# Token shift of the delta rule: two VectorE passes and an accumulating transfer in place of a copy and three passes

## The chip, the cores and the metric

The kernel runs on one core of a Trainium2 chip. The metric is the time of one launch in microseconds on the device, the median of several runs. TensorE does the matrix products, VectorE, ScalarE and GpSimd the work element by element, and SyncE and the queues of ScalarE and GpSimd issue transfers. Each engine, and each queue, takes its instructions in order; they wait for one another through semaphores.

## What is computed

Two blocks follow one another on 256 tokens of 1024 columns: a first block of attention and a mixture of experts, and a second block of two layers, each with three mixers. One of these is a delta rule (RWKV-7). Its inputs r, k, v and two narrow ones are shifted: each token's row is mixed with the row of the token ahead of it, by a weight mu of its own for each column.

```python
prev = jnp.pad(shift_cols, ((0, 0), (1, 0), (0, 0)))[:, :-1]
shifted = shift_cols + rwkv_mu[l] * (prev - shift_cols)
r, k, v, wl, al = split_cols(shifted, RWKV_SIZES)
```

For the first token prev is zero. r, k and v have 512 columns each, and the two narrow ones 64 each, 128 together.

## The kernel before

The 256 tokens lie on 128 partitions as two tiles (TT = 2): a tensor of 512 columns is 128 x 1024 numbers, token t on partition t modulo 128 in tile t // 128. One token further on is therefore one partition further on, and from partition 127 of the first tile to partition 0 of the second. [...]

The shifts are made in `shift_mix` (L1722). It is called four times in each layer: from `mix_in` for the narrow pair (mx, n = 128), and from `shifted` for k, r and v (n = 512). `shifted` loads the row mu by SyncE (`bc_row`), has `copy_chunk` compute the 512 columns p on TensorE and bring them out of PSUM with ScalarE (L1480), and calls `shift_mix` with the buffer prev. There a GpSimd memset (L1725) clears the first token's row, three transfers from ScalarE's queue (`Q_SHIFT = "scalar"`, L1727 and L1728: 112 partitions, 15 partitions and the one row that changes tile) copy p into prev one token on, and three VectorE passes (L1729 to L1731) form prev − p, times mu, plus p. Then prev and mu are given back to the slots from which they were taken, and others use the space.

Around that, TensorE streams the second block's other weights. Each 512-column weight tile is split in two parts for TensorE: wh on ScalarE (L460) and wl on VectorE (L461), and three products L503, L504 and L505 use them. The next consumers of the shifted tensors are: for mx the transposes and a tanh on ScalarE; for k VectorE's L1716; for r L1876; for v TensorE's products L2025 in the first layer, whose 64 x 256 parts are also moved by GpSimd's queue (L2067), and in the second layer transposes L549 and a mix with the first layer's v, L2013. The first layer's v is stored by GpSimd's queue (vfirst).

The order on each engine comes from generators that are woven together: `rwkv_prep` runs in a lane of priority 30 beside attention and the gated products (`drive`, `weave`, with ratios R0 to R6), and a scheduler places instructions by these priorities and by when their inputs come. A change in one routine therefore also moves its neighbours.

Of the kernel before, what the change touches and what calls it, by code (L numbers as in the profile page):

```python
# [13 lines left out]
ALU = mybir.AluOpType  # L14
# [3 lines left out]
P = 128  # L18
S = 256
TT = 2  # L20
# [17 lines left out]
Q_SHIFT = "scalar"  # L38
# [371 lines left out]
class Net:  # L410
# [1311 lines left out]
    def shift_mix(self, p, prev, mu, n, eng):  # L1722

        nc = self.nc
        nc.gpsimd.memset(prev[0:1, 0], 0.0)  # L1725
        for a, b in ((0, 112), (112, P - 1)):
            self.q(Q_SHIFT).dma_start(out=prev[a + 1:b + 1], in_=p[a:b])  # L1727
        self.q(Q_SHIFT).dma_start(out=prev[0:1, 1], in_=p[P - 1:P, 0])  # L1728
        eng.tensor_tensor(prev, prev, p, op=ALU.subtract)  # L1729
        eng.tensor_tensor(prev, prev, mu[:, None, :].to_broadcast([P, TT, n]), op=ALU.mult)  # L1730
        eng.tensor_tensor(p, p, prev, op=ALU.add)  # L1731

    def mix_in(self, l):

# [525 lines left out]
```

## Time and profile before

| | us |
|---|---|
| median of 3 runs | 1532.31 (1531.42 to 1538.03) |
| the profiled execution | 1529.58 |
| its span | 1527.7 |
| TensorE busy | 1444.2 |
| VectorE busy | 866.3 |
| ScalarE busy | 580.7 |
| GpSimd busy | 72.3 |

The profiled execution is one launch recorded on the chip; the span is from its first to its last instruction. Busy times are summed per engine, and issues of transfers are not counted as busy. In a timeline a row begins with its start and its duration in us, and the bracket at its end tells how long the engine was idle before it, and what released it. ACTq is ScalarE's queue of issues. The first block ends, and the second begins, at about 700 us; the first layer's shifts lie at 729 (mx), 783 (k), 848 (r) and 882 us (v), the second's at 1135, 1187, 1249 and 1279.

### The profile page before, as it was taken

What the parts mean: (1) busy time and instruction counts of PE and PEld (TensorE: products, weight loads), DVE (VectorE), ACT (ScalarE), POOL (GpSimd) and SP (SyncE); (2) the same over time, 40 slices, a digit from 0 to 9 for tenths busy, and PEclk for the clock granted to TensorE, in tenths of its full rate; (3) what the DMA queues carried; (4) which work ended last, traced back from release to release, by engine and by line L of the source; (5) the groups of instructions that cost most, each with busy time, mean ns of one, the idle gap of its engine ahead of it and who ended that gap; (6) DMA issues with size and microseconds to landing.
All of it is one profiled execution on the core that took longest, in us unless ns stands there. A gap on an engine that the chain in (4) does not pass through costs nothing.

```text
span 1527.7 us, 23577 instructions
## 1 busy us (share of the span) xinstructions
PE 1444.2 (95%) x9314; PEld 995.6 (65%) x9314; DVE 866.3 (57%) x1773; ACT 580.7 (38%) x1164; POOL 72.3 (5%) x90
## 2 busy tenths in 40 slices
PE   9998999989999999987998989999999998999997
PEld 8886444435985444436667668777776775787776
DVE  6664322226765232227757777476776687855665
ACT  6543111103441110105455442355455564325553
POOL 0023000001000000003000010000100000000001
PEclk9998999999999999999999999999999998999999
DMA  9853999999654999997134342134454454112443
GB/s 354 331 216 132 421 421 420 421 421 419 258 200 165 421 421 421 421 421 264 42 127 151 122 139 68 63 144 170 162 196 143 138 173 151 68 37 72 167 180 119
DMA packets 56569, 350.69 MB, mean 230 GB/s; under 512 B 7434, under 2 KB 8456, under 8 KB 17030
## 3 DMA queue, kind: packets, MB, share of 16 engines
q1 hardware_dynamic: 51542, 335.61, 56.6%
q0 software_dynamic: 2112, 8.03, 1.6%
q10 hardware_dynamic: 2800, 5.49, 1.4%
q8 instruction: 75, 1.23, 0.3%
q14 instruction: 40, 0.33, 0.1%
HBM read 338.90 MB, written 3.67 MB: 224 GB/s over the span
## 4 chain that ended last, share of the span: by engine, by line
PE 42%; DVE 6%; DMA 2%; ACT 2%; issue 1%; ACTq 0%; DVEq 0%
PE ps_h L504 5%; PE ps_h L503 5%; PE ps_g L504 5%; PE ps_h L505 4%; PE ps_g L503 4%; PE ps_g L505 4%; PE ps_a L2025 4%; PE ps_b L2025 3%; PE ps_a L549 1%; DVE wl L461 1%; DMA arena<-arena_x 1%; PE ps_a L1523 1%; ACT wh L460 1%; PE ps_b L1523 1%; PE ps_b L1546 1%
## 5 line engine op out<-in xcount | busy, mean ns | idle before, releaser
L461 DVE TENSOR_TENSOR wl<-w_w,wh 128x512 fp32r<-128x512 f32 (+1 forms) x338 | 225.0, 682 | 128.5 <-ACT wh L460 127.1
L460 ACT ACTIVATE wh<-w_w 128x512 fp32r<-128x512 f32 (+1 forms) x350 | 212.4, 625 | 209.3 <-PE ps_g L505 98.5
L1118 PE MATMUL ps_g<-w_x,xe 128*64 128x512 f32 x456 | 145.4, 594 | 8.1 <-DMA w_x<-in_moe_dram 8.1
L1118 PE MATMUL ps_g<-w_e,xe 128*64 128x512 f32 x440 | 142.4, 594 | 3.8 <-DMA w_e<-in_moe_dram 3.8
L504 PE MATMUL ps_h<-wl,hh 128*128 128x512 f32 (+2 forms) x272 | 109.6, 407 | 5.9 <-DVE wl L461 5.9
L504 PE MATMUL ps_g<-wl,hh 128*128 128x512 f32 (+2 forms) x272 | 108.9, 405 | 1.7 <-DVE wl L461 1.6
L503 PE MATMUL ps_g<-wh,hh 128*128 128x512 f32 (+2 forms) x272 | 103.3, 404 | 5.0 <-ACT wh L460 3.4
L503 PE MATMUL ps_h<-wh,hh 128*128 128x512 f32 (+2 forms) x272 | 104.3, 406 | 3.0 <-ACT wh L460 2.1
L505 PE MATMUL ps_h<-wh,hlo 128*128 128x512 f32 (+2 forms) x272 | 106.8, 395 | 0.0
L505 PE MATMUL ps_g<-wh,hlo 128*128 128x512 f32 (+2 forms) x272 | 105.4, 391 | 0.0
L1128 DVE SCALAR_TENSOR_TENSOR eg<-eg,ps_g 128x512 f32<-128x512 f32 x16 | 11.0, 687 | 157.8 <-ACT eg L1127 157.8
L1118 PEld LDWEIGHTS ps_g<-w_x,xe 128*64 128x64 f32 x456 | 45.1, 137 | 74.3 <-issue 58.0
L1118 PEld LDWEIGHTS ps_g<-w_e,xe 128*64 128x64 f32 x440 | 44.9, 137 | 68.7 <-issue 60.4
L1127 ACT ACTIVATE eg<-ps_g 128x512 f32<-128x512 f32 x16 | 9.6, 597 | 176.8 <-PE ps_g L1118 176.8
L1154 DVE SCALAR_TENSOR_TENSOR wl<-ps_g,slotw,wh 128x512 fp32r<-128x512 f32 x32 | 24.0, 751 | 92.4 <-ACT wh L1153 92.4
L460 ACT ACTIVATE wh<-w_x 128x512 fp32r<-128x512 f32 (+1 forms) x92 | 55.5, 615 | 52.5 <-PE ps_g L522 20.9
L1150 PE MATMUL ps_g<-w_e,eg 128*64 128x512 f32 x248 | 72.3, 596 | 0.0
L1153 ACT ACTIVATE wh<-ps_g,slotw 128x512 fp32r<-128x512 f32 x32 | 22.0, 687 | 121.7 <-PE ps_g L1150 121.7
L504 PEld LDWEIGHTS ps_h<-wl,hh 128*128 128x128 f32 x272 | 52.1, 192 | 24.6 <-DVE wl L461 13.9
L504 PEld LDWEIGHTS ps_g<-wl,hh 128*128 128x128 f32 x272 | 51.9, 191 | 19.0 <-DVE wl L461 10.5
L503 PEld LDWEIGHTS ps_g<-wh,hh 128*128 128x128 f32 x272 | 50.6, 191 | 20.6 <-ACT wh L460 10.5
L503 PEld LDWEIGHTS ps_h<-wh,hh 128*128 128x128 f32 x272 | 50.6, 192 | 19.9 <-ACT wh L460 9.8
(792 smaller groups left out, 3163.7 us busy)
## 6 DMA issues: line engine op xcount, KB each, us to landing
w_e<-in_moe_dram SPq DMA_DIRECT2D x86, 1024.0 KB, 19.7
w_x<-in_moe_dram SPq DMA_DIRECT2D x79, 1024.0 KB, 19.7
w_w<-in_win_dram SPq DMA_DIRECT2D x57, 1024.0 KB, 4.8
w_w<-in_moe_dram SPq DMA_DIRECT2D x27, 1024.0 KB, 19.2
w_x<-in_wkv_dram SPq DMA_DIRECT2D x8, 1024.0 KB, 14.0
w_w<-in_wo_dram SPq DMA_DIRECT2D x8, 1024.0 KB, 4.8
w_x<-in_winb_dram SPq DMA_DIRECT2D x6, 1024.0 KB, 19.8
w_e<-in_wout_dram SPq DMA_DIRECT2D x4, 1024.0 KB, 17.4
```

The costliest lines, as they stand in the source:

```text
L460: self.nc.scalar.activation(hi, src, AF.Copy)
L461: self.q(eng).tensor_tensor(lo, src, hi.bitcast(F32), op=ALU.subtract)
L503: nc.tensor.matmul(o, xh[:, kk, ts], wh[:, k], start=f, stop=False)
L504: nc.tensor.matmul(o, xh[:, kk, ts], wl[:, k], start=False, stop=False)
L505: nc.tensor.matmul(o, xl[:, kk, ts], wh[:, k], start=False, stop=e)
L549: nc.tensor.transpose(ps[:rows, b, tt * P:tt * P + P], src[:, tt, (b0 + b) * rows:(b0 + b + 1) * rows], self.C("ident"))
L1118: nc.tensor.matmul(gu[m][es], xe[:, kk, pr % 2, es], w[e][:, k], start=kk == 0, stop=kk == KD - 1)
L1150: nc.tensor.matmul(yp[es], hT[:, k, es], w[e][:, k], start=k == 0, stop=k == 3)
L1153: nc.scalar.activation(yh, yp, AF.Identity, scale=wt)
L1154: v.scalar_tensor_tensor(yl, yp, wt, yh.bitcast(F32), op0=ALU.mult, op1=ALU.subtract)
L1523: nc.tensor.matmul(s[:, h], qT[:, h0 + h, tt * P:tt * P + P], kT[:, h0 + h, :nk], start=True, stop=False)
L2025: ins = self.nc.tensor.matmul(out, lhsT, rhs, start=start, stop=stop)
```

## The change

The function forms p·mu in prev and takes it off p, and then adds prev to p one token on by the transfers themselves. The first token gets nothing added, so no memset is needed. The transfers leave ScalarE's queue for GpSimd's and accumulate in their destination. They now read prev and write p, and prev is free only after them; mu is free after the first pass.

```diff
     def shift_mix(self, p, prev, mu, n, eng):

         nc = self.nc
-        nc.gpsimd.memset(prev[0:1, 0], 0.0)
+        eng.tensor_tensor(prev, p, mu[:, None, :].to_broadcast([P, TT, n]), op=ALU.mult)
+        eng.tensor_tensor(p, p, prev, op=ALU.subtract)
         for a, b in ((0, 112), (112, P - 1)):
-            self.q(Q_SHIFT).dma_start(out=prev[a + 1:b + 1], in_=p[a:b])
-        self.q(Q_SHIFT).dma_start(out=prev[0:1, 1], in_=p[P - 1:P, 0])
-        eng.tensor_tensor(prev, prev, p, op=ALU.subtract)
-        eng.tensor_tensor(prev, prev, mu[:, None, :].to_broadcast([P, TT, n]), op=ALU.mult)
-        eng.tensor_tensor(p, p, prev, op=ALU.add)
+            nc.gpsimd.dma_start(out=p[a + 1:b + 1], in_=prev[a:b], accum_op=ALU.add)
+        nc.gpsimd.dma_start(out=p[0:1, 1], in_=prev[P - 1:P, 0], accum_op=ALU.add)
```

Lines behind the function stand two lower in the changed kernel: L1725 and L1726 are its passes, L1728 and L1729 its transfers, and L1874 is the L1876 of before. In the rows below, arena and xres are the large buffers out of which slots are cut, the number is the slot's; DMAHW are semaphores of transfers from SyncE's and ScalarE's queue, DMASW those of transfers from GpSimd's.

VectorE at k of the second layer, before: p is arena_x_5737, mu is in arena_x_5788 and prev in arena.

```order
L461 TENSOR_TENSOR wl<-w_w_9799,wh 128x512 [waits DMAHW6_49,Activation_49]
L1729 TENSOR_TENSOR arena<-arena,arena_x_5737 128x1024 [waits DMAHW1_49,DMAHW2_49,DMAHW0_49,Activation_49]
L461 TENSOR_TENSOR wl<-w_w_9799,wh 128x512 [waits PE_49,Activation_49]
L1730 TENSOR_TENSOR arena<-arena,arena_x_5788 128x1024 [waits DMAHW5_49,DVE_49]
L1550 TENSOR_TENSOR arena<-ps_b,at_sm_9863 128x256 [waits PE_49]
L1528 TENSOR_REDUCE at_mx_9932<-ps_b 128x2 [waits PE_49]
L1731 TENSOR_TENSOR arena_x_5737<-arena_x_5737,arena 128x1024 [waits DVE_49]
L1716 SCALAR_TENSOR_TENSOR arena<-xres,arena 128x1024 [waits DMAHW3_49]
L1533 RECIPROCAL at_sm_9933<-at_sm_9933 128x2 [waits Activation_49]
L461 TENSOR_TENSOR wl<-w_w_9799,wh 128x512
L1716 SCALAR_TENSOR_TENSOR arena<-arena,arena_x_5737 128x1024 [waits DVE_49]
```

The same place with the change; p is arena_x_5735 here.

```order
L1725 TENSOR_TENSOR arena<-arena_x_5735,arena_x_5786 128x1024 [waits DMAHW6_49,DMAHW3_49,Activation_49]
L461 TENSOR_TENSOR wl<-w_w_9789,wh 128x512 [waits PE_49,Activation_49]
L1726 TENSOR_TENSOR arena_x_5735<-arena_x_5735,arena 128x1024 [waits DVE_49]
L1533 RECIPROCAL at_sm_9921<-at_sm_9921 128x2 [waits Activation_49]
L461 TENSOR_TENSOR wl<-w_w_9789,wh 128x512 [waits PE_49,Activation_49]
L461 TENSOR_TENSOR wl<-w_w_9866,wh 128x512 [waits DMAHW1_49,Activation_49]
L1550 TENSOR_TENSOR arena<-ps_b,at_sm_9921 128x128 [waits DVE_49,PE_49]
L1528 TENSOR_REDUCE at_mx_10029<-ps_b 128x2 [waits PE_49]
L461 TENSOR_TENSOR wl<-w_w_9866,wh 128x512 [waits Activation_49]
L1716 SCALAR_TENSOR_TENSOR arena<-arena,arena_x_5735 128x1024 [waits DMASW4_49,DMASW3_49,DMASW2_49]
```

The wait for the transfers has moved from the first pass to L1716, the consumer of the shifted k, and six rows stand between the last pass and it, with one more wl between the two passes.

ScalarE at the same place, before; rows "DMA" are issues.

```order
L1480 ACTIVATE arena_x_5737<-ps_h,h_y 128x512 [waits DMAHW4_49,PE_49]
L1480 ACTIVATE arena_x_5737<-ps_h,h_y 128x512 [waits PE_49]
L1728 DMA arena<-arena_x_5737 1x16x32 [waits Activation_49]
L1727 DMA arena<-arena_x_5737 112x1024 [waits Activation_49]
L1727 DMA arena<-arena_x_5737 15x1024 [waits DMAHW2_49]
L1480 ACTIVATE arena_x_5737<-ps_g,h_y 128x512 [waits PE_49] x2
L460 ACTIVATE wh<-w_w_9799 128x512 [waits DVE_49]
L460 ACTIVATE wh<-w_w_9799 128x512 x2
```

And with the change; L1805 writes into the slot that prev had.

```order
L1480 ACTIVATE arena_x_5735<-ps_h,h_y 128x512 [waits DMAHW5_49,PE_49]
L1480 ACTIVATE arena_x_5735<-ps_h,h_y 128x512 [waits PE_49]
L460 ACTIVATE wh<-w_w_9789 128x512 [waits DVE_49]
L1531 ACTIVATE arena_x_5786,at_sm_9921<-ps_b,at_mx_9920 128x256 [waits DMAHW6_49,DMAHW3_49,DVE_49]
L1531 ACTIVATE arena_x_5786,at_sm_9921<-ps_b,at_mx_9920 128x256
L1480 ACTIVATE arena_x_5735<-ps_g,h_y 128x512 [waits PE_49]
L1541 COPY arena_x_5786<-ps_b 128x512 [waits PE_49,Activation_49]
L460 ACTIVATE wh<-w_w_9789 128x512
L460 ACTIVATE wh<-w_w_9866 128x512 [waits DMAHW1_49,PE_49]
L460 ACTIVATE wh<-w_w_9866 128x512 [waits PE_49]
L1805 ACTIVATE arena<-ps_a 128x512 [waits DMASW3_49,DMASW2_49,DVE_49]
```

The three issues are gone from ahead of the eviction L1480 of the other tile and of wh; L1805 now waits for the three transfers.

TensorE at v of the second layer, before: the last products ahead of the transposes of v (L549, reading arena_x_5737), 35 products behind the last one of the v chunk (wh, hh).

```order
L503 MATMUL ps_g<-wh,c_r_10446 128x512 [waits Activation_49]
L503 MATMUL ps_g<-wh,c_r_10446 128x512
L504 MATMUL ps_g<-wl,c_r_10446 128x512 [waits DVE_49]
L505 MATMUL ps_g<-wh,c_r_10447 128x512
L503 MATMUL ps_h<-wh,c_r_10446 128x512 [waits Activation_49]
L504 MATMUL ps_h<-wl,c_r_10446 128x512
L504 MATMUL ps_g<-wl,c_r_10446 128x512
L505 MATMUL ps_h<-wh,c_r_10447 128x512
L505 MATMUL ps_g<-wh,c_r_10447 128x512
L549 MATMUL ps_a<-consts_108,arena_x_5737 128x128 [waits DVE_49,PE_49]
```

And with the change, from the third product behind the v chunk's last one on.

```order
L503 MATMUL ps_h<-wh,c_r_10434 128x512 [waits Activation_49]
L504 MATMUL ps_h<-wl,c_r_10434 128x512
L505 MATMUL ps_h<-wh,c_r_10435 128x512
L503 MATMUL ps_g<-wh,c_r_10434 128x512 [waits Activation_49]
L503 MATMUL ps_g<-wh,c_r_10434 128x512
L504 MATMUL ps_g<-wl,c_r_10434 128x512 [waits DVE_49]
L505 MATMUL ps_g<-wh,c_r_10435 128x512
L504 MATMUL ps_g<-wl,c_r_10434 128x512
L505 MATMUL ps_g<-wh,c_r_10435 128x512
L549 MATMUL ps_a<-consts_108,arena_x_5735 128x128 [waits DMASW0_49,DMASW1_49,DVE_49,PE_49]
L549 MATMUL ps_a<-consts_108,arena_x_5735 128x128 [waits Activation_49]
L549 MATMUL ps_a<-consts_108,arena_x_5735 128x128 [waits DMASW2_49]
```

The transposes wait for the transfers themselves, with 12 products behind the v chunk's last one. At v of the first layer the products L2023 (L2025 before) wait likewise, behind 31 products of 512 columns and 18 small ones.

## Rows read from the trace of the kernel before

**Rows 1.** The page: busy time by engine, and the chain by engine.

```profile
PE 1444.2 (95%) x9314; PEld 995.6 (65%) x9314; DVE 866.3 (57%) x1773; ACT 580.7 (38%) x1164; POOL 72.3 (5%) x90
PE 42%; DVE 6%; DMA 2%; ACT 2%; issue 1%; ACTq 0%; DVEq 0%
```

**Rows 2.** Stretches: start:end, us, busy by engine (rows), granted clock, DMA share, GB/s.

```profile
700.00:1528.00 828.00, 775.96 (x5768) 597.03 (x5766) 562.66 (x1128) 393.24 (x821) 39.53 (x59) 0.98 0.38 128
1195.00:1200.00 5.00, 3.73 (x12) 2.35 (x11) 5.00 (x8) 3.48 (x9) 0.00 (x0) 0.67 0.01 3
1440.00:1480.00 40.00, 40.00 (x172) 29.46 (x171) 23.64 (x36) 21.66 (x37) 0.00 (x0) 1.00 0.49 179
```

**Rows 3.** TensorE's timeline around the shifts.

```profile
732.65 0.50 PE L503 MATMUL ps_h<-wh,hh 128*128 128x512 f32 x1 [0.78 <-ACT wh L460]
...
785.82 0.50 PE L503 MATMUL ps_h<-wh,hh 128*128 128x512 f32 x1 [1.29 <-ACT wh L460]
...
851.40 0.50 PE L503 MATMUL ps_g<-wh,hh 128*128 128x512 f32 x1 [1.40 <-ACT arena_x L1420]
...
884.45 0.49 PE L503 MATMUL ps_g<-wh,c_r 128*128 128x512 f32 x1 [0.33 <-ACT wh L460]
...
897.52 0.68 PE L2025 MATMUL ps_a<-arena_x,arena 64*64 64x64 f32 x16 [1.14 <-DVE arena_x L1731]
...
1189.70 0.43 PE L1546 MATMUL ps_b<-arena_x,arena 128*128 128x64 f32 x2 [1.32 <-ACT arena_x L1480]
...
1194.27 0.50 PE L504 MATMUL ps_g<-wl,hh 128*128 128x512 f32 x1 [0.70 <-DVE wl L461]
...
1196.99 0.69 PE L1538 MATMUL ps_b<-consts,arena_x 128*128 128x128 f32 x2 [1.27 <-ACT arena_x L1531]
...
1285.48 0.50 PE L503 MATMUL ps_h<-wh,c_r 128*128 128x512 f32 x1 [0.68 <-ACT arena_x L1664]
...
1290.06 0.50 PE L503 MATMUL ps_h<-wh,c_r 128*128 128x512 f32 x1 [2.17 <-ACT arena L1420]
...
1294.24 1.94 PE L549 MATMUL ps_a<-consts,arena_x 128*128 128x128 f32 x8 [2.76 <-DVE arena_x L1731]
```

**Rows 4.** VectorE's timeline at k of both layers.

```profile
788.63 1.23 DVE L1729 TENSOR_TENSOR arena<-arena,arena_x 128x1024 f32<-128x1024 f32 x1 [1.04 <-DMA arena<-arena_x]
...
789.89 1.22 DVE L1730 TENSOR_TENSOR arena<-arena,xres 128x1024 f32<-128x1024 f32 x1
...
791.03 0.68 DVE L461 TENSOR_TENSOR wl<-w_w,wh 128x512 fp32r<-128x512 f32 x1
...
791.63 1.22 DVE L1731 TENSOR_TENSOR arena_x<-arena_x,arena 128x1024 f32<-128x1024 f32 x1
...
1192.39 1.23 DVE L1729 TENSOR_TENSOR arena<-arena,arena_x 128x1024 f32<-128x1024 f32 x1 [5.88 <-DMA arena<-arena_x]
```

**Rows 5.** ScalarE's timeline at k of the first layer.

```profile
783.02 0.54 ACTq L1728 DMA_DIRECT2D arena<-arena_x  x1
...
783.66 1.43 ACTq L1727 DMA_DIRECT2D arena<-arena_x  x2
```

**Rows 6.** Issues of transfers: engine, count, KB each, median us to landing.

```profile
xsave<-xres POOLq DMA_DIRECT2D x2, 1024.0 KB, 5.5
...
vfirst<-arena_x POOLq DMA_DIRECT2D x1, 512.0 KB, 3.2
...
arena_x<-arena_x ACTq DMA_DIRECT2D x1, 448.0 KB, 3.7
...
xres<-arena_x ACTq DMA_DIRECT2D x1, 448.0 KB, 5.2
```

**Rows 7.** GpSimd's queue, and VectorE's timeline, behind v of the first layer.

```profile
899.58 0.52 POOL L2067 DMA_DIRECT2D arena<-arena_x  x1
...
900.59 0.58 POOL L1890 DMA_DIRECT2D vfirst<-arena_x  x1
...
899.71 0.68 DVE L461 TENSOR_TENSOR wl<-w_w,wh 128x512 fp32r<-128x512 f32 x1
```

## The prediction

> **What bounds the kernel now.** I began with the page. TensorE is busy 1444.2 of 1527.7 us, and the chain that ended last is mostly TensorE, with 6% VectorE and 2% DMA [rows 1]. A change on VectorE, ScalarE's queue and GpSimd's queue therefore pays only where TensorE stands idle for it. All eight shifts lie in the second block, 700 to 1528 us, where TensorE is busy 775.96 of 828 us [rows 2]: 52 us of idle in all, shared by everything. Next I read TensorE's timeline around each shift, keeping the bracket at a row's end, the idle time before it and what released it [rows 3]; then VectorE's and ScalarE's timelines there [rows 4, 5]; then what transfers take [rows 6, 7].
>
> The reader is to see three sorts of idle that belong to the shifts. (a) ScalarE issues the three transfers itself: at the first layer's k it issues from 783.02 to 785.09 [rows 5], with the next weight conversion wh queued behind; TensorE waits 1.29 us for that wh until 785.82 [rows 3]. The same thing is 0.78 us at 732.65 (first mix) and 1.32 us at 1189.70 (second layer's k, where an eviction, L1480, stands behind the issues). (b) VectorE stands still until the transfer lands: 5.88 us at 1192.39, 1.04 at 788.63 [rows 4]. After the long one TensorE idles 0.70 and 1.27 us (1194.27, 1196.99). (c) TensorE waits for the shifted v itself, L1731: 1.14 us at 897.52 and 2.76 at 1294.24 [rows 3]. Together 0.78+1.29+1.32+0.70+1.27+1.14+2.76 = 9.3 us. That is about all that the old shift costs TensorE directly; two idles beside it (1.40 at 851.40 by an eviction, 2.17 at 1290.06) belong to it in part or not at all.
>
> Idle has a second price. From 1195 to 1200, behind the idle at the second k, the granted clock is 0.67 [rows 2]: a part of the stretch at 1.2 instead of 2.4 GHz, a third of 5 us, some 1.6 us of clock time. The stretch 1440 to 1480 shows the undisturbed engine: clock 1.00, busy 40.00 us, 172 large matmuls or 0.23 us each [rows 2]. I count up to 1.6 us for each k and the second v as gain or loss with the idle, but only in the bounds.
>
> **The change part by part.**
>
> *Removed: one VectorE pass per shift.* A large pass is 1.22 to 1.23 us [rows 4], and a mix has a quarter of its columns: 6 x 1.22 + 2 x 0.3 = 7.9 us of VectorE. VectorE isn't the bound, and the row count of the rest is unaltered, so by itself this is worth nothing; it counts only through the time at which p is ready.
>
> *Removed: 24 issues on ScalarE's queue.* Per shift about 2.07 us of queue time (783.02 to 785.09). Idle (a) goes: 0.78+1.29+1.32 = −3.4 us. I take −3.2, since a wh that comes sooner meets the next wait within some tenths. The 8 GpSimd memsets lie on an almost idle queue: nothing.
>
> *Added: 24 accumulating transfers from GpSimd's queue.* An issue there takes 0.52 us (uv, 899.58) to 0.58 (vfirst) [rows 7]; GpSimd's issues follow one another, so three take 1.6 us. Behind them stand the uv transfers after v, which need v anyway, and vfirst, needed a layer later. The landing is the unknown: no transfer of the trace accumulates. Lower bound: the plain 512 KB from GpSimd, 3.2 us; the old 448 KB copy took 3.7 to 5.2. An accumulation also reads its destination, so twice the traffic: the 1 MB transfers from GpSimd took 5.5 [rows 6]. A price well above twice the copy can't be excluded: 2 x 5.2 = 10.4 as upper end. I take 5.5, by the 1 MB row, as the nearest in bytes touched.
>
> The Trainium skill (DMA: Bandwidth & Descriptors, Anatomy of one DMA — SWDGE (gpsimd) path) gives a GpSimd transfer 2.0 us plus bytes over 436 GB/s, an estimate of 3.05 us for 448 KB; the vfirst row, 3.2 us for 512 KB, agrees. It prices no accumulation; with 3.05 as landing the sum below would be about −13 us.
>
> *Moved: where the landing is waited for.* Before, it stood between eviction and the first pass; now behind two passes. From eviction to p ready: before, at the first k, 783.66 (issue of the large copy, right behind the eviction) to 792.85 (end of L1731), 9.2 us [rows 4, 5]. Now pass, one wl (0.68) between, pass, issue and landing: 1.14+0.60+1.14+0.5+5.5 = 8.9 us (rows of VectorE follow at 1.14 and 0.60, as 789.89, 791.03, 791.63 show). So p is ready at about the same time; what differs is who waits, with what cover.
> - k, both layers. The order puts 6 rows between L1726 and L1716, which waits for the landing: a reciprocal, three wl, and the pair L1550 and L1528, an estimated 2.9 us by three wl of 0.68 and three short ones. VectorE then waits 0.5+5.5−2.9 = 3.1 us, against 1.04 and 5.88 before. Also new: ScalarE's L1805 writes the slot that prev had, so ScalarE waits for the same landing, with wh queued behind it. Long waits of 5.88 cost TensorE 0.70+1.27 = 2.0, 0.34 us per us; with ScalarE held too I take half: 2 x 1.5 = +3.0, against −2.0 that goes. Net +1.0.
> - r, both. L1874 (L1876 before) waits, behind about 9 rows of VectorE, some 5 us: 0 to 1 us of wait each, cost +0.3; the eviction at 851.40 loses half of its 1.40 with the issues gone: −0.7. Net −0.4.
> - v of the first layer. TensorE's product L2023 waits for the landing itself, with some 31 large matmuls ahead of it, 7.2 us. Evictions 1.3, then 8.9, make 10.2 after the chunk's last matmul: a wait of 3.0. Before, that stretch holds seven idles, the first at 884.45 and the last at 897.52 [rows 3], 4.8 us, of which ScalarE's issues and the late v are most. Net −1.5.
> - v of the second layer. The order moves the chunk later against TensorE's other work: 12 matmuls, 2.8 us, stand between its last one and the transposes L549 that wait for the landing, where 35 stood before. Wait 10.2−2.8 = 7.4 us, against four idles before, the first at 1285.48 and the last at 1294.24 [rows 3]: 0.68+0.24+2.17+2.76 = 5.85. Net +1.5.
> - mix, both. A quarter of the bytes, and VectorE has rows of another chain between its passes and the consumer. Nothing beyond the −0.8 counted in (a).
>
> Sum: −3.2 +1.0 −0.4 −1.5 +1.5 = −2.6 us, on the profiled execution's 1529.58: 1527.0. The median of the three runs, 1532.31, lies 2.7 above it, so 1529.7; I say 1529. Per us of landing beyond 5.5, k costs 2 x 0.8, r 0.7, v 2: some 4.3 us. Zero change lies at a landing of about 6.1.
>
> **The rivals.**
> - *The accumulation is slow.* One mechanism: its landing takes the copy's twice or more, 8 to 10.4 us, and VectorE, ScalarE (k, r) and TensorE (v) stand for the rest. At 9: −2.6+3.5 x 4.3 = +12 us, 1545; it decides from 6.1 and is measurable (7.7 us) from about 8. For it: SBUF copies of 448 KB already took up to 5.2; against: 1 MB takes 5.5.
> - *VectorE starves GpSimd's transfers.* Passes behind L1726 would hold descriptors back; then a landing grows by the pass under way, 0.68, once or several times: 0.7 to 2 us, +3 to +9 us, 1533 to 1538. Against: issues of uv stayed at 0.52 us beside a VectorE pass at 899.71 [rows 7]. The Trainium skill (SBUF — State Buffer, SBUF: two separate sides) warns of this for VectorE's two-port modes and would leave such transfers on ScalarE's or SyncE's queue, where they were. I see two-input passes beside these issues, not its fp32 copies, so the trace only half tests it.
> - *All old idles go.* Landing 3.2 to 4.2: −2.6−1.3 x 4.3 to −2.6−2.3 x 4.3, −8 to −12.5, 1520 to 1524; with the clock dips gone some 3 more. For it: the vfirst row.
> - *Nothing measurable because the scheduler's new order decides.* Rows from 4700 on are reshuffled in the second layer's tail as well; ±4 us about zero. This lies within the forecast's range.
>
> **How the numbers follow.** Forecast (landing 4.5 to 7): 0.46, its own range 1524 to 1536. Slow accumulation: 0.22. Starved: 0.08. All idles go: 0.24. A measurement of this kernel can tell about 0.5%, 7.7 us, from no change. Faster by more: the third rival nearly whole, with a little of the forecast, 0.26. Slower by more: most of the slow case and a third of the starved one, and a little of the forecast, 0.27. Same: 0.47. Range: down to 1518 and up to 1547 (landing 9 to 9.5), which leaves 0.1 at either side.
>
> **What would show it.** The landing of the 448 KB transfer on GpSimd's queue, first of all: under 4.5 the gain, over 8 the loss. VectorE's wait at L1716: 3 us in each k. ScalarE's wait at L1805. TensorE's wait before L2023 in the first v (3.0) and L549 in the second (7.4). The idles (a) gone, with 24 rows off ScalarE's queue, and the clock in each k's stretch. The prediction is wrong if the landing is far from 5.5, or if TensorE's idle in 700 to 1528 (52 us) moves at places without a shift.

## The result, and the profile after

The changed kernel takes 1556.24 us (1549.43 to 1558.34, 4 runs) against 1533.85 of the kernel before in the same runs: a ratio of 1.0142, with a 95% interval of 1.0119 to 1.0165. It is slower by 1.4%, some 22 us. The forecast was 1529, with a range of 1518 to 1547; the time lies 9 us above the range. The profiled execution of the changed kernel took 1558.34 us, with a span of 1556.4. It is the slowest of its four runs, and the profiled one of the kernel before (1529.58) is faster than all four of its runs; so the two pages lie 28.8 us apart, more than the 22 of the medians.

The page of the changed kernel, busy time by engine; it answers to the first row of [rows 1]:

```profile
PE 1453.9 (93%) x9314; PEld 1000.6 (64%) x9314; DVE 859.7 (55%) x1765; ACT 581.0 (37%) x1164; POOL 89.8 (6%) x106
```

VectorE has 6.6 us less (7.9 were expected from the pass that went), and GpSimd 17.5 more, since the page counts issues on GpSimd's own queue as busy, unlike those on the others. TensorE is busy 9.7 us longer with the same 9314 products. The second block by itself, in the columns of [rows 2]:

```profile
700.00:1556.00 856.00, 785.95 (x5776) 602.54 (x5776) 558.81 (x1125) 395.81 (x824) 59.05 (x77) 0.96 0.38 125
```

The block's stretch grew from 828 to 856 us. TensorE's idle in it grew from 52.0 to 70.1, by 18 us; the other 10 us are busy time, at a mean granted clock of 0.96 instead of 0.98. So TensorE waits more, and the same products take it longer; e5 below tells how much of either is the accumulation's. Where it waits stands in TensorE's timeline; the rows are those of the places in [rows 3]:

```profile
802.08 2.07 PE L1808 MATMUL ps_a<-arena_x,consts 128*128 128x512 f32 x2 [5.41 <-ACT arena L1806]
...
866.41 1.06 PE L503 MATMUL ps_h<-wh,hh 128*128 128x512 f32 x2 [3.05 <-ACT wh L460]
...
1153.58 0.69 PE L549 MATMUL ps_a<-consts,arena_x 128*128 128x128 f32 x2 [4.43 <-ACT arena_x L1779]
...
1221.10 2.07 PE L1808 MATMUL ps_a<-xres,consts 128*128 128x512 f32 x2 [5.82 <-ACT arena L1806]
...
1288.26 0.73 PE L503 MATMUL ps_g<-wh,hh 128*128 128x512 f32 x2 [3.13 <-ACT wh L460]
...
1320.18 2.28 PE L549 MATMUL ps_a<-consts,arena_x 128*128 128x128 f32 x8 [7.65 <-DMA arena_x<-xres]
```

Six waits, 29.5 us in all: at both k (802.08, 1221.10) behind ScalarE, at both r (866.41, 1288.26) behind a conversion wh, at the second layer's mix (1153.58) behind ScalarE's tanh, and at the second layer's v (1320.18) directly behind the transfer. At the first v, TensorE waits 2.8 us for the transfer in the view of waits. The idles behind ScalarE's issues, at 732.65, 785.82 and 1189.70 in [rows 3], are gone.

The transfers, in the columns of [rows 6]:

```profile
arena_x<-arena POOLq DMA_DIRECT2D x3, 448.0 KB, 5.9
...
arena_x<-arena_x POOLq DMA_DIRECT2D x1, 448.0 KB, 6.4
...
arena_x<-arena POOLq DMA_DIRECT2D x3, 60.0 KB, 9.9
...
arena_x<-arena_x POOLq DMA_DIRECT2D x1, 112.0 KB, 7.2
...
arena_x<-arena POOLq DMA_DIRECT2D x3, 2.0 KB, 9.6
...
xres<-arena POOLq DMA_DIRECT2D x1, 2.0 KB, 7.6
```

The large transfer lands 5.9 us after its issue. But the 60 KB behind it take 9.9, and the single row of 2 KB 9.6, and VectorE at k and r waits for the last of the three. GpSimd's queue and VectorE at the first k tell the same in time, from the second pass on:

```profile
790.36 1.65 POOL L1728 DMA_DIRECT2D arena_x<-arena  x2 [52.54 <-ACT xres L1541]
...
791.44 1.39 POOL L1729 DMA_DIRECT2D arena_x<-arena  x1
```

```profile
788.59 1.22 DVE L1726 TENSOR_TENSOR arena_x<-arena_x,arena 128x1024 f32<-128x1024 f32 x1
...
795.47 0.69 DVE L461 TENSOR_TENSOR wl<-w_w,wh 128x512 fp32r<-128x512 f32 x1 [2.00 <-ACT wh L460]
...
801.16 1.23 DVE L1716 SCALAR_TENSOR_TENSOR arena<-arena,arena_x 128x1024 f32<-128x1024 f32 x1 [5.00 <-DMA arena_x<-arena]
```

The second pass ends at 789.81. The first transfer is issued at 790.36; L1716 starts at 801.16, 11.3 us behind the pass. The rows of the three issues overlap: they start 0.56 and 0.52 us apart, as often as plain ones (0.52 in [rows 7]), though each row lasts longer.

### The profile page after: what moved, and what is told of

It is laid out like the page before. It is cut to its first block, busy times and chain, and to the rows that moved or that the text cites. A ratio compares the mean times of both kernels' runs of the same rounds, so it can differ in the third digit from the quotient of the medians.

```text
span 1556.4 us, 23547 instructions
## 1 busy us (share of the span) xinstructions
PE 1453.9 (93%) x9314; PEld 1000.6 (64%) x9314; DVE 859.7 (55%) x1765; ACT 581.0 (37%) x1164; POOL 89.8 (6%) x106
## 5 line engine op out<-in xcount | busy, mean ns | idle before, releaser
L504 PEld LDWEIGHTS ps_h<-wl,hh 128*128 128x128 f32 x272 | 52.3, 192 | 22.5 <-DVE wl L461 11.9
```

The source lines that it names most:

```text
L504: nc.tensor.matmul(o, xh[:, kk, ts], wl[:, k], start=False, stop=False)
```

## The experiments

All times below are compared with the kernel before by runs on the same chip; a ratio under 1 is faster than before.

**The tail of the transfers (e1, e2).** Theory A: the small transfers are late because they queue behind the large one, so another split helps. Theory B: the accumulation takes its time whatever the split.

```diff
-        for a, b in ((0, 112), (112, P - 1)):
-            nc.gpsimd.dma_start(out=p[a + 1:b + 1], in_=prev[a:b], accum_op=ALU.add)
+        nc.gpsimd.dma_start(out=p[1:P], in_=prev[0:P - 1], accum_op=ALU.add)
```

> One accumulating transfer of 127 partitions takes the place of the two of 112 and 15; the one row that changes tile stays. In the changed kernel the 448 KB transfer landed in 5.7 to 6.4 us, but the 60 KB one behind it in 6.4 to 10.4 and the last row in 6.8 to 10.1, and the consumers wait for the last. Theory A (the tail: the small transfers queue behind the large one on the same engines, and behind the weights): the large transfer lands in 6.5 us, the last row perhaps 8; each k loses 1.5 to 3 us less, the time falls by 5 to 10 us, to some 1547. Theory B (the accumulation is slow as such, whatever the split): the 508 KB transfer itself lands in 9 to 10 us and the time stays within 3 us of 1556.

Measured: 1567.26 us, ratio 1.0231 (1.0193 to 1.0270), slower still than the change itself.

```profile
arena_x<-arena POOLq DMA_DIRECT2D x3, 508.0 KB, 7.5
...
arena_x<-arena POOLq DMA_DIRECT2D x3, 2.0 KB, 9.6
```

The 508 KB land in 7.5 us and the row in 9.6, 0.54 us later by issue: p is whole 10.1 us after the first issue at k, against 10.7 with three. Theory A's landings (6.5 and 8) didn't come, and neither did theory B's (9 to 10 for the 508 KB); the time is above both ranges.

e2 turns the order round: the row, then 15 partitions, then 112.

```diff
+        nc.gpsimd.dma_start(out=p[0:1, 1], in_=prev[P - 1:P, 0], accum_op=ALU.add)
-        for a, b in ((0, 112), (112, P - 1)):
+        for a, b in ((112, P - 1), (0, 112)):
             nc.gpsimd.dma_start(out=p[a + 1:b + 1], in_=prev[a:b], accum_op=ALU.add)
-        nc.gpsimd.dma_start(out=p[0:1, 1], in_=prev[P - 1:P, 0], accum_op=ALU.add)
```

> The same three accumulating transfers, the single row first, then 15 partitions, then 112. Theory A: the small ones land in 3 us, the large one in about 6.5 from its own issue, and the last landing comes 7.5 to 8 us after the first issue instead of 10.7: 1546 to 1550. Theory B: the same last landing, 10 us or more after the first issue, and the time stays within 3 us of 1556.

Measured: 1567.31 us, ratio 1.0252 (1.0198 to 1.0306).

```profile
arena_x<-arena POOLq DMA_DIRECT2D x3, 448.0 KB, 9.2
...
arena_x<-arena POOLq DMA_DIRECT2D x3, 60.0 KB, 5.1
...
arena_x<-arena POOLq DMA_DIRECT2D x3, 2.0 KB, 1.9
```

Now the row lands in 1.9 us, the 60 KB in 5.1 and the 448 KB in 9.2: the last one is late again, and it is the large one. Theory A's cure fails: at k the whole takes 10 to 11 us after the first issue in any split or order. What stood ahead of the large one at the first k is seen in the transfer engines from 789 to 792 us (packets, MB, share of the engines; q1 is SyncE's queue, q0 GpSimd's):

```profile
q1 hardware_dynamic: 101, 0.83, 86.3%
q0 software_dynamic: 32, 0.06, 11.4%
```

It was a weight load of 1 MB, which SyncE had issued at 787.10, 0.2 us behind the large transfer. In the changed kernel the load was issued at 791.58, behind all three: there the large transfer went first, the load next, and the small ones along with the load. So at k a transfer that comes late shares the engines with that load; at the first mix, where no weight load is beside, the third lands 2.5 us after its issue. No run moves the load alone.

That both kernels are 11 us slower than the change by their medians (0.9% and 1.1% by their ratios) isn't explained by landings, which hardly differ. Nor is it idle time: behind 700 us TensorE idles 71.5 and 73.1 us in their traces, against 70.1, but is busy 793.3 and 791.0, against 786.0. The order of the other instructions differs from that of the change; what moved the busy time stays open.

**No transfers at all (e3).**

```diff
-        for a, b in ((0, 112), (112, P - 1)):
-            nc.gpsimd.dma_start(out=p[a + 1:b + 1], in_=prev[a:b], accum_op=ALU.add)
-        nc.gpsimd.dma_start(out=p[0:1, 1], in_=prev[P - 1:P, 0], accum_op=ALU.add)
```

> The two passes stay and the transfers are left out, so the shifted token is missing from the sum. Nobody waits for a landing. If the landing is the whole of the loss, this runs some 8 to 14 us below the kernel before, 1520 to 1526, since the old waits are gone too (9.3 us of idle). If the order of the work on TensorE and ScalarE is a part of the loss (rival), it stays at or above 1532.

Measured: 1514.12 us, ratio 0.9885 (0.9854 to 0.9916). The sum then lacks the shifted token; it is a kernel for timing only. The two passes alone lose nothing, and with the order that this kernel got, a shift without transfers is worth 1.2%, some 18 us, more than the 9.3 us of idle that the prediction counted. In its trace most of that is not idle: behind 700 us TensorE idles 45.5 us instead of 52.0, and is busy 765.5 instead of 776.0, at a mean granted clock of 0.99 instead of 0.98.

**The queue or the accumulation (e4).** The kernel before, its copies issued by GpSimd.

```diff
-Q_SHIFT = "scalar"
+Q_SHIFT = "gpsimd"
```

> The kernel before with its three plain copies issued from GpSimd's queue instead of ScalarE's; three passes as before. It tells the queue from the accumulation. If the accumulation is what is slow (A and B), the plain copies land in 3 to 5 us, the last one too, issues take 0.5 us, and the time is 1528 to 1535: ScalarE's idles (3.4 us) go, and the scheduler's order moves the rest by some us. If GpSimd's queue is slow as such (rival), the last copy lands in 8 to 10 us and the time is 1545 to 1555.

Measured: 1520.41 us, ratio 0.9920 (0.9889 to 0.9950): faster than the kernel before, and beyond what was expected (1528 to 1535).

```profile
arena<-arena_x POOLq DMA_DIRECT2D x3, 448.0 KB, 4.3
...
arena<-arena_x POOLq DMA_DIRECT2D x3, 60.0 KB, 4.5
...
arena<-arena_x POOLq DMA_DIRECT2D x3, 2.0 KB, 3.5
```

The same bytes from the same queue, without accumulation, land in 4.3, 4.5 and 3.5 us. GpSimd's queue as such is not slow. TensorE's idle behind 700 us is 51.9 us, as before (52.0); the trace has the gain in busy time, 770.5 instead of 776.0.

**The accumulation alone (e5).** The sharpest test: the changed kernel without the one argument, so that the transfers write over p instead of adding to it. On VectorE, ScalarE and TensorE the order of instructions is the same, row for row.

```diff
-            nc.gpsimd.dma_start(out=p[a + 1:b + 1], in_=prev[a:b], accum_op=ALU.add)
-        nc.gpsimd.dma_start(out=p[0:1, 1], in_=prev[P - 1:P, 0], accum_op=ALU.add)
+            nc.gpsimd.dma_start(out=p[a + 1:b + 1], in_=prev[a:b])
+        nc.gpsimd.dma_start(out=p[0:1, 1], in_=prev[P - 1:P, 0])
```

> The changed kernel with the accumulation taken off its three transfers: they write prev over p instead of adding it, so the sum is left out. Every instruction, its order and its waits are those of the changed kernel. Theory B (accumulating transfers of GpSimd's queue are slow and run one behind another): the last landing comes about 5.5 us after the first issue, as in e4, instead of 10.7; the wait at L1716 falls from 5 to about 1 us in each k, and the time to 1525 to 1535. Rival (the two-pass order itself loses, wherever the landing): 1545 or more, with the waits still 3 us or longer.

Measured: 1540.51 us, ratio 1.0023 (1.0002 to 1.0043). Against the changed kernel's 1.0142 the accumulation is 1.2%, 18 of the 22 us (the two ratios come from different sets of runs). The view of issues:

```profile
arena_x<-arena POOLq DMA_DIRECT2D x3, 448.0 KB, 3.7
...
arena_x<-arena POOLq DMA_DIRECT2D x3, 60.0 KB, 5.7
...
arena_x<-arena POOLq DMA_DIRECT2D x3, 2.0 KB, 6.0
```

And TensorE's and VectorE's timeline at the first k, where the changed kernel has 5.41 and 5.00:

```profile
795.86 1.13 PE L1808 MATMUL ps_a<-arena_x,consts 128*128 128x512 f32 x2 [1.21 <-ACT arena L1806]
```

```profile
795.52 1.23 DVE L1716 SCALAR_TENSOR_TENSOR arena<-arena,arena_x 128x1024 f32<-128x1024 f32 x1 [1.38 <-DMA arena_x<-arena]
```

Plain, the last of three lands 7 us after the first issue (1.05 + 6.0) and not 10.7; the 5.5 that was expected is missed too, so a tail behind the large transfer is there without accumulation, only shorter. TensorE's wait at the first k falls from 5.41 to 1.21 us, and at the second from 5.82 to 1.84. The other four of the six waits, in order of time (first r, second mix, second r, second v; the changed kernel has 3.05, 4.43, 3.13 and 7.65):

```profile
856.93 0.74 PE L503 MATMUL ps_h<-wh,hh 128*128 128x512 f32 x2 [1.28 <-ACT wh L460]
...
1142.56 0.69 PE L549 MATMUL ps_a<-consts,arena_x 128*128 128x128 f32 x2 [4.50 <-ACT arena_x L1779]
...
1273.21 0.73 PE L503 MATMUL ps_g<-wh,hh 128*128 128x512 f32 x2 [1.79 <-ACT wh L460]
...
1304.29 1.94 PE L549 MATMUL ps_a<-consts,arena_x 128*128 128x128 f32 x8 [6.33 <-DMA arena_x<-xres]
```

As the rows correspond one to one, the accumulation can be priced place by place: 8.2 us at the two k, 3.1 at the two r, 1.9 at the two v (0.6 and 1.3) and nothing at the second mix, 13.2 us of idle in these two executions, which lie 15.6 us apart. The stretch as a whole:

```profile
700.00:1540.80 840.80, 784.83 (x5776) 602.27 (x5776) 558.02 (x1125) 395.12 (x824) 50.72 (x77) 0.97 0.38 127
```

TensorE is busy 784.8 us here, against 786.0 with the accumulation and 776.0 before. So the accumulation costs idle time; the 10 us of busy time belong to what this kernel shares with the change, its order above all, or come from which execution was profiled before.

The time is 5 us above the expected range, and 0.2% above the kernel before: the order of this kernel has its own waits, 4.5 us at the second mix and 6.3 at the second v, which stay without accumulation. There the prediction's 7.4 us at L549 comes mostly from the order, not from the accumulation.

What the engines of the transfers do is seen in stretches of 1 us at the first k, behind the issue. The columns are those of [rows 2]; the last two are the share of the transfer engines and what they moved. In the changed kernel all of it is of GpSimd's queue; in e5 that holds for the first stretch, and in the second the next weight load has begun. First the changed kernel, then e5:

```profile
791.40:792.40 1.00, 1.00 (x10) 0.95 (x9) 0.76 (x2) 0.00 (x0) 1.00 (x2) 1.00 0.83 123
792.40:793.40 1.00, 1.00 (x7) 0.87 (x7) 0.82 (x2) 0.00 (x0) 0.43 (x1) 1.00 1.04 139
```

```profile
789.90:790.90 1.00, 1.00 (x7) 0.90 (x7) 0.58 (x3) 0.00 (x0) 0.02 (x1) 1.00 0.94 242
790.90:791.90 1.00, 1.00 (x6) 0.80 (x5) 0.55 (x1) 0.00 (x0) 0.00 (x0) 1.00 1.02 262
```

In both, the transfer engines are full or nearly so (0.83 to 1.04, the records' ends being rough). They move 123 to 139 GB/s with the accumulation and 242 to 262 without: about half the rate, with little of the engines left for others. The weight load that SyncE issues next lands the later for it. At the first k, 9.1 us after its issue in the changed kernel and 7.6 in e5:

```profile
w_w<-in_win_dram SPq DMA_DIRECT2D x1, 1024.0 KB, 9.1
```

```profile
w_w<-in_win_dram SPq DMA_DIRECT2D x1, 1024.0 KB, 7.6
```

In the kernel before, the load at that place took 4.8. At the first r it is 8.4 with the accumulation and 6.6 without.

**ScalarE's wait for the slot (e6).** The prediction had ScalarE's L1805 wait for the slot of prev; here prev is held longer.

```diff
-        self.sl.put(prev, mu)
+        self.sl.put(mu)
+        if nm == "k":
+            self.held_prev = prev
+        else:
+            self.sl.put(prev)
...
         dp, dm, di, de = big("dp"), big("dm"), big("di"), big("de")
+        sl.put(self.held_prev)
```

> The changed kernel, with k's prev given back only after dp, dm, di and de have taken their space, so that ScalarE's L1805 no longer writes the slot that the transfers read. Theory: in each k TensorE stood 5.4 and 5.8 us for L1806 behind that wait; without it ScalarE goes on, VectorE still waits at L1716, and TensorE loses 1 to 3 us at each k: 1546 to 1552. Rival (VectorE's wait alone does it): no change, 1553 to 1560.

Measured: 1561.66 us, ratio 1.0161 (1.0112 to 1.0210): no gain. At the two k TensorE's waits did fall, from 5.41 and 5.82 us to 3.65 and 3.88, though not to the 1 to 3 that were expected; but this kernel's order has other waits (10.42 us at 1336), and its idle behind 700 us is 70.5, the same as the change's. So the whole time doesn't tell what the slot is worth. ScalarE's timeline at the first k shows what came behind the slot, and the changed kernel's at the first r, where there is no such slot, shows the same:

```profile
799.17 0.63 ACT L460 ACTIVATE wh<-w_w 128x512 fp32r<-128x512 f32 x1 [3.91 <-DMA w_w<-in_win_dram]
```

```profile
865.73 0.63 ACT L460 ACTIVATE wh<-w_w 128x512 fp32r<-128x512 f32 x1 [3.32 <-DMA w_w<-in_win_dram]
```

ScalarE, freed from the slot, waits 3.91 us for a weight load w_w. At r in the changed kernel it waits 3.32 us for one, and TensorE idles the 3.05 us seen at 866.41. By e5 the accumulation's part of that idle is 1.8 us, and 1.3 at the second r. It holds the engines that the weights need: a cost to those who never asked for p. No term of the prediction had it.

**Idle accumulations (e9, e10).** To price that by itself, each k gets three transfers more that nobody waits for, on top of the copies of e8 (below): plain in e9, accumulating in e10, with the same order (but for one pair of products in the first block).

```diff
+        if nm == "k":
+            for a, b in ((0, 112), (112, P - 1)):
+                self.nc.gpsimd.dma_start(out=prev[a + 1:b + 1], in_=t[a:b], accum_op=ALU.add)
+            self.nc.gpsimd.dma_start(out=prev[0:1, 1], in_=t[P - 1:P, 0], accum_op=ALU.add)
+            self.held_prev = prev
```

> The kernel of e8 (plain copies from SyncE's queue) with prev held at k until dp to de have their space, and at each k three plain copies more from GpSimd's queue, of the shifted k into the dead prev, for which nobody waits. It is the control of e10: within 5 us of e8's 1514.

> As e9, but the three idle transfers at each k accumulate. Every instruction and wait stands as in e9, and nobody waits for these transfers. Theory C (accumulations hold the transfer engines, so that the weight loads of SyncE's queue land later, as the wait of ScalarE for w_w in e6 showed): weight loads beside them land 1.5 to 2.5 us later and the time is 2 to 8 us above e9. Rival (the cost lies only with those who wait for p): within 2 us of e9.

Measured: e9 1526.65 us, ratio 0.9965 (0.9942 to 0.9987); e10 1532.01, ratio 1.0001 (0.9979 to 1.0023). The pair differs by 0.36%, 5.4 us, for two shifts' accumulations that nobody waits for; the intervals overlap a little. ScalarE's waits for these weights, e9 first, then e10 (total us, times, longest):

```profile
ACT wh L460 <- DMA w_w<-in_win_dram: 1.4, 1, 1.4
```

```profile
ACT wh L460 <- DMA w_w<-in_win_dram: 5.4, 3, 3.2
```

They grow by 4.0 us, but only one of the three, 3.2 us at 811.7, stands behind the idle accumulations; the load there landed 7.6 us after its issue instead of 7.0, less than the 1.5 to 2.5 us more that were expected. TensorE's waits behind the two shifts grow by 2.25 us (1.62 to 2.39 at the first k; 0.39 to 1.38 and 0 to 0.49 at the second). The two profiled executions can't tell more: they took 1531.53 and 1532.35 us, only 0.8 us apart, e9's being 5 us above its median. So the times agree with theory C, and the traces show less than half of the price. The control itself missed: e9 was expected within 5 us of e8 and is 1% slower. It has the held prev, six plain transfers more and another order, with two idles of TensorE of 8 us at v of the second layer and behind it; what each of these costs wasn't separated. So two kernels of different order can differ by more than the mechanism in question, and only pairs of equal order (the change and e5, e9 and e10) price it finely.

**SyncE's queue (e8) and one copy of 127 (e7).** Two other homes for the plain copies.

```diff
-Q_SHIFT = "scalar"
+Q_SHIFT = "sync"
```

> The kernel before with its three plain copies issued from SyncE's queue. It takes them off ScalarE as e4 does, but SyncE's queue also issues the weight loads, each of which waits for its buffer. If leaving ScalarE is the whole of e4's gain, this comes to 1518 to 1526 too. If copies stand behind weight loads there, or weight loads behind copies that wait for an eviction, 1530 to 1545.

Measured: 1513.99 us, ratio 0.9863 (0.9832 to 0.9894). It is the fastest whole kernel of the study, 1.4% ahead of before. The copies land as before:

```profile
arena<-arena_x SPq DMA_DIRECT2D x3, 448.0 KB, 4.3
...
arena<-arena_x SPq DMA_DIRECT2D x3, 60.0 KB, 4.1
```

At the first k, VectorE's L1729 starts without waiting, and TensorE idles 0.24 us in all from 775 to 800:

```profile
790.91 0.69 DVE L461 TENSOR_TENSOR wl<-w_w,wh 128x512 fp32r<-128x512 f32 x1 [0.49 <-ACT wh L460]
...
791.52 1.22 DVE L1729 TENSOR_TENSOR arena<-arena,arena_x 128x1024 f32<-128x1024 f32 x1
```

The copies are the same, so leaving ScalarE's queue, with the order that follows from it, is worth far more than the 3.2 us that the prediction allowed. How much of it is ScalarE's time and how much the order wasn't separated; behind 700 us TensorE idles 44.0 us, and is busy 768.0, 8 us less of either than before. e7 is e4 with one copy of 127 partitions:

```diff
-        for a, b in ((0, 112), (112, P - 1)):
-            self.q(Q_SHIFT).dma_start(out=prev[a + 1:b + 1], in_=p[a:b])
+        self.q(Q_SHIFT).dma_start(out=prev[1:P], in_=p[0:P - 1])
```

> The kernel of e4 (three passes, plain copies from GpSimd's queue) with one copy of 127 partitions in place of 112 and 15. If GpSimd's queue spreads 127 partitions as it spreads 112, it lands in 4.3 to 4.8 us, the shift is complete 0.7 us earlier than in e4, and the time is 1516 to 1521. If such a copy is spread badly it lands in 8 us or more and the time is above 1530.

Measured: 1524.12 us, ratio 0.9928 (0.9903 to 0.9952), the same as e4 by the intervals, and 3 us above the expected range. The copies of 508 KB landed in 4.4 to 4.7 us, as expected; it wasn't worth anything that can be measured.

**The change at one place (e11, e12).** On top of e8, accumulation at k alone, and at r alone.

```diff
-        self.shift_mix(t, prev, mu, 512, eng)
+        self.shift_mix(t, prev, mu, 512, eng, nm == "k")
```

> The kernel of e8, with the change at k alone, in both layers (two passes and accumulating transfers from GpSimd's queue); the other six shifts keep the plain copies from SyncE's queue. In the changed kernel TensorE lost 5.4 and 5.8 us there. If that is the price of the place: 8 to 14 us above e8, 1522 to 1528. If the places only lose together (rival): within 4 us of e8.

> As e11, with the change at r alone. There nine rows of VectorE stand between the last pass and the consumer, and TensorE lost 3.1 us in each layer behind wh in the changed kernel. If the cover does what the prediction said (0.3 us lost, 2.4 us of VectorE saved): within 3 us of e8, 1511 to 1517. If the transfer engines are held against the weight loads: 4 to 8 us above e8.

Measured: e11 1548.02 us, ratio 1.0096 (1.0059 to 1.0133); e12 1517.39, ratio 0.9900 (0.9871 to 0.9930). The change at k alone takes e8's whole gain and 1% more. That is 34 us by the medians, where 8 to 14 were expected. TensorE's view of waits shows 11.9 of them directly at the two k:

```profile
PE ps_a L1817 <- ACT arena L1815: 11.9, 2, 6.2
```

The two profiled executions lie 37.5 us apart. Of the rest, 15 us are busy time of TensorE behind 700 us (783.2 against 768.0 in e8), at a mean granted clock of 0.96 instead of 0.98, and some 10 are idle at places with another order, in waits of up to 8.2 us; what moved either stays open. At r alone it is 0.4% slower than e8 by the ratios, some 6 us, though the intervals overlap. That lies in the range of the second theory (4 to 8 us) rather than of the first (within 3), and ScalarE's wait for weights points the same way, 9.4 us against 4.2 in e8. But the two have different orders, and the difference isn't clear of the noise: whether the change does harm at r alone wasn't settled.

## Why the prediction was wrong, point by point

*The forecast's step that failed is the landing.* The landing of the large transfer was predicted at 5.5 us and measured at 5.6 to 6.4; that term was near. But the working took it for the landing of the shift. Its "0.5+5.5" for issue and landing counts one transfer out of three. From the end of the second pass to L1716 it was 11.3 us at the first k, not 6.0: 0.55 to the first issue, and 10.7 until the last of three had landed. The old shift had not shown it: its three, plain and from ScalarE's queue, had all landed within 5.5 us of their issues where the trace tells. Of the 5.2 us that 10.7 has more than the 5.5, e5 puts 3.6 down to the accumulation (7.0 plain, in the same order) and 1.5 to a tail that plain transfers have there too. The prediction summed the issues of all three, but asked for the landing of only one, and its first sign of being wrong, the landing of the 448 KB, was as blind: 5.9 us is neither under 4.5 nor over 8. The term that it put at nothing is the other traffic: a weight load on the same engines at k and r, for which TensorE idled 3.05 and 3.13 us at r.

*The sum with the right landing is near by luck.* With the 5.2 us that k's last landing had more, the prediction's 4.3 us for each us beyond 5.5 give 1529.7 + 5.2 x 4.3 = 1552, and the measured median is 1556.2. So the first rival, "the accumulation is slow", is what happened, in kind and at k also in size; its landing was bounded per transfer, at 8 to 10.4, and its chance of 0.22 was too low. But the sum agrees because errors cancel: it charges 10.4 us to the two v, where 1.4 came, and nothing to the mix, where 4.4 came; r cost 5.8 and not 3.2; and of the 28 us by which the profiled stretch grew, 10 are busy time, which it leaves out.

*k.* Predicted +3.0 us for both, by half of VectorE's wait. Measured: 5.41 and 5.82 us of TensorE's idle. The wait was 5.0 and 5.4 us on VectorE instead of 3.1, and TensorE lost all of it and not half; without the accumulation TensorE's wait is 1.21 and 1.84. Both feeders of TensorE stood for the same transfer, ScalarE at L1805 for 5.5 and 5.9 us. Yet e6 shows that the slot was no more than the first in line: without it TensorE still lost 3.65 and 3.88 us, for ScalarE then waited for weights.

*r.* Predicted +0.3 and −0.7. Measured 3.05 and 3.13 us of idle behind wh. VectorE's wait for the landing was 2.8 us each, the cover being short by that much; but TensorE waited for ScalarE, which waited for a weight load. By e5 the accumulation's part is 1.8 and 1.3 us; the rest is there with plain transfers too. This term wasn't in the prediction.

*v.* Predicted waits of 3.0 and 7.4 us; measured 2.8 and 7.65. Both are right in size, and both by luck in part. At the first v TensorE went on at 900.23, when the large transfer alone had landed (900.10); the last landed at 903.64, while other products ran. At the second, L549 began 7.7 us behind the second pass and not 6.0; but the 12 products that cover it took 4.6 us and not 2.8, with two idles of 0.41 and 0.88 among them, and the two errors cancel. That wait is now known to be mostly the order's: it is 6.3 without accumulation. That the cover could be read off the order, 12 products instead of 35, was the best step of the working. The 5.85 us that it set against this wait took in the 2.17 at 1290.06, which its own list had put down as not the shift's, or only in part.

*mix.* Predicted: nothing. Measured: 4.43 us at the second layer, behind ScalarE's tanh, which waits 6.34 us for transfers of 112 KB. They land in 7.2 us there, with a weight load of 1 MB beside them in the trace, and the idle stays at 4.5 without accumulation (e5): this one is not the accumulation's but, by the trace, the meeting of two transfers in the new order. In the kernel before, that load was issued at 1137.15, just ahead of the landing of the shift's first copy, which took 2.2 us. A quarter of the bytes was no price for it.

*Removed: ScalarE's issues and the pass.* The idles went, as predicted. e4 and e8 show that moving the copies, with the order that follows, is worth more than the 3.2 us taken: 0.8% and 1.4%. The change gave that away again.

*Starved descriptors.* The second rival doesn't show. The Trainium skill (SBUF — State Buffer, SBUF: two separate sides) warns of VectorE, in its two-port modes, holding up GpSimd's transfers; in e4 all 24 issues on GpSimd's queue took 0.50 to 0.57 us and landed as ScalarE's had, so by this trace it cost nothing that shows. No experiment put a long fp32 copy of VectorE beside them.

*Clock.* The stretch's mean granted clock fell from 0.98 to 0.96, and TensorE's busy time rose by 10 us. The prediction kept that out of its sum and in the bounds; beside 18 us of idle, 10 is no small print. But e5, without the accumulation's waits, is busy as long (784.8 us), so they aren't its cause; what is stays open.

## What to carry to other kernels

When a copy becomes an accumulating transfer, price the last landing of all its parts, not the largest one's, and ask what else needs the transfer engines meanwhile. An accumulation here ran them at half the rate, and the weights behind it paid. Before making a shift cheaper in arithmetic, try to take its issues off the engine that feeds TensorE: one word in the source (e8) was worth 1.4%, the whole rewrite cost as much. And compare mechanisms in pairs of equal order, row by row: here kernels of another order moved by 10 us and more for reasons that weren't found.

## What the runs showed of the hardware that was not expected

Of three accumulating transfers, whichever was issued last landed 9 to 10 us after its issue at k, be it 2 KB (9.6) or 448 KB (9.2); in the same order plain ones took 3.7, 5.7 and 6.0 us, accumulating ones 5.9, 9.9 and 9.6. A weight load of 1 MB was on the engines beside them each time; without one, at the first mix, an accumulating shift of a quarter of the bytes was whole 3.6 us after its first issue. Accumulating transfers moved 123 to 139 GB/s with the engines full or nearly so, against 242 for plain ones in the stretch that has them alone, and the weight load behind them landed 9.1 us after its issue, against 7.6. The row of an accumulating issue on GpSimd's queue lasts longer the later it comes: 0.83 to 0.90 us for the first of three, 1.09 to 1.18 for the second and 1.39 to 1.47 for the third, against 0.50 to 0.57 for plain ones. In e2, where the single row comes first, it is the one with 0.77 to 0.84. But the rows overlap, and the issues start 0.52 to 0.58 us apart in the change as in e5 (0.51 to 0.55).
